# Interleaved high and low parts of split weights, and other start places of the token rows, in a hybrid decoder layer

## The chip, the cores and the metric

The kernel runs on one core of one Trainium2 chip. The metric is device time in microseconds (us) of one execution, the median of several runs. The core has five engines that run side by side: TensorE (PE in the profile; its weight loads are shown apart as PEld), VectorE (DVE), ScalarE (ACT), GpSimd (POOL) and SyncE (SP), which here only starts transfers. Sixteen DMA engines move data between HBM and the on-chip memory, which has 128 partitions. TensorE writes its results into accumulator banks (PSUM), from which VectorE and ScalarE take them.

## The reference

One layer of a decoder, for 4096 new tokens of one sequence and 8 times 8 sampled tokens, all float32 with a model width of 1024:

```
h = rmsnorm(x) * g_pre
z = h @ w_in                  # 1024 x 2816, columns for three groups
A: silu(cg) * cb * conv3(cc * ch)                      # gated short convolution, 256 channels
B: silu(ag) * window attention(q, k, v; sink)          # 8 query heads, 2 key heads, window 128
C: silu(mg) * cross attention(mq; 256 memory tokens)   # 4 heads
y = concat(A, B, C) @ w_out   # 1024 x 1024
x + rmsnorm(y) * g_post
```

Beside y for both sets of tokens it returns the last keys, values and convolution inputs, and the memory's keys and values. The kernel keeps float32 accuracy in the large products.

## The kernel before

**Split operands.** [...] A product of two such operands is three matmuls: high with high, high weight with low row, low weight with high row; the product of the two low parts is left out. `product` (line 370) makes them for one 128-wide group of output columns, 260 token columns and the four 128-deep slices of one half of the model width: 12 matmuls, all issued by line 375, each with a weight load of its own. The weights are the operand that is loaded into the array (128 columns), the token rows are streamed through it (260 columns).

**Input projection, 0 to about 935 us.** The 4160 tokens are cut into 8 blocks of 520, and the 22 groups of 128 columns of `w_in` into 11 pairs, which are treated in three phases: four pairs in each of the first two, three in the last. In most blocks a block and a pair are multiplied by a scheme with seven products in place of eight (Strassen's, Winograd's form), for which sums and differences of the weights and of the rows are made ahead; the first two blocks of the first phase use the eight plain products instead. A step is one product of the scheme for all pairs of the phase. In each step TensorE runs 48 matmuls (36 in the third phase), VectorE and ScalarE add the results into the z tiles (`evict`, line 378), and the operand of the next step is split (`split`, line 363: the high part on ScalarE, line 365, the low part on VectorE, line 366). In the third phase attention work of the first tokens stands between the products.

**Where the operands lie.** Each weight tile has 128 partitions and in each of them 1024 numbers, the 512 high parts and then the 512 low parts (`w_slot`, line 174). The tiles of the first three pairs come from the pool `wa`, those of the fourth from the pool `wb`. In the built program the tiles of `wa` begin at a multiple of 256 bytes, those of `wb` 32 bytes below one. `w_split` (line 181) fills a tile: ScalarE casts the high parts (line 182), VectorE subtracts (line 186). In the first phase 17 operations of VectorE (line 605) put whole weights together again from both parts. The split rows lie in tiles of four slices with 320 numbers each, 1280 bytes or five times 256, of which 260 are used. Where in the 320 they begin is set by `begins` (line 355): for two steps that follow each other, the high parts begin 8 or 16 numbers (32 or 64 bytes) and the low parts 40 or 48 numbers (160 or 192 bytes) in. All tiles of rows begin at a multiple of 256 bytes.

**The rest, 935 us to the end.** Attention units and the output projection (line 1501) alternate on TensorE. In the output projection the token rows are the loaded operand, and the weights `wo` are streamed, 512 columns at a time. The tiles of `wo` are made on line 908, in the same pool `wa`, but not by `w_slot`: they are filled by `w_split` too.

The order of the work on each engine is the order in which the program is written where `tc.keep_in_program_order` or the manual schedule holds it, and a scheduler's elsewhere.

Of the kernel before, what the change touches and what calls it, by code (L numbers as in the profile page):

```python
# [9 lines left out]
F32R = mybir.dt.float32r  # L10
# [5 lines left out]
P = 128  # L16
# [36 lines left out]
def hybrid_layer(ctx: ExitStack, tc: tile.TileContext, a: dict):  # L53
# [30 lines left out]
    wa = ctx.enter_context(tc.tile_pool(name="wa", bufs=3 * NP_))  # L84
    pa = ExitStack()
    wb_stack = ExitStack()
    wb = wb_stack.enter_context(tc.tile_pool(name="wb", bufs=NP_, side="right"))
# [84 lines left out]
        return tp.tile([P, wide + 2 * HW], F32, tag="t", name=name)  # L172

    def w_slot(qi, name):
        return (wa if qi < 3 else wb).tile([P, 2, 512], F32R, tag="w", name=name)

    def w_raw(pair, o):

# [173 lines left out]
                tc.keep_in_program_order(ins)  # L352
            store(hd[b][o], ops[o])

    begins = {"hi": [8, 16], "lo": [40, 48]}

    def split_tile(tag, name):

# [239 lines left out]
    def first_fill(o, q, raw=None):  # L598
        ws[0, q, o] = w_slot(q, f"w0_{q}{o}")
        w_split(ws[0, q, o], raw0.pop((q, o)) if raw is None else raw)  # L600
# [273 lines left out]
    def next_fill(nph, q, o):  # L874
        ws[nph, q, o] = w_slot(q, f"w{nph}_{q}{o}")
        w_split(ws[nph, q, o], raws.pop((q, o)))
# [815 lines left out]
```

## Time and profile before

| | before |
|---|---|
| median of 3 runs | 1540.98 us (1539.1 to 1541.51) |
| profiled execution, and its span | 1543.23 us, 1541.5 us |
| mean granted TensorE clock | 0.998 |
| PE, PEld, DVE, ACT, POOL busy | 99%, 91%, 74%, 52%, 25% of the span |
| matmuls of the input projection (line 375) | 7488, 54.7% of the chain of waits |
| matmuls of the output projection (line 1501) | 22.5% of the chain of waits |

The profile gives for every instruction its engine, its source line, its start and its length. Matmuls are pipelined: the length of one (282 ns for 260 columns) holds its way through the array and says little of the rate, which is read from the distance between the starts of two, or from a stretch of the chain of waits over many. The chain of waits follows the work that ended last back to what released it, and so names what set the time at each moment. PEclk is the share of TensorE's clock that was granted in a stretch.

### The profile page before, as it was taken

Reading aid. Unit: us, or ns where it says so; the run is one execution under the profiler, and the core shown is the slowest. Engines: PE = TensorE matmul, PEld = TensorE weight load, DVE = VectorE, ACT = ScalarE, POOL = GpSimd, SP = SyncE. Lnnn points to the kernel's source line nnn. Section 1 sums busy time; section 2 is a strip of 40 time slices with the busy share of each in tenths; the row PEclk is TensorE's granted clock in tenths of the full one; section 3 lists DMA queues with packets and bytes.
Section 4 is the critical chain, followed back from the end, with each engine's and each line's share of the span. In section 5 each row is a group of like instructions: output and inputs, shape, how many; then the busy total and the mean of one; then the engine's idle time right before and its main releaser. Section 6 shows DMA issues by size and latency. Waiting matters only on the chain.

```text
span 1541.5 us, 30150 instructions
## 1 busy us (share of the span) xinstructions
PE 1529.6 (99%) x11331; PEld 1407.2 (91%) x11331; DVE 1147.0 (74%) x2055; ACT 806.8 (52%) x2039; POOL 380.8 (25%) x604
## 2 busy tenths in 40 slices
PE   9999999999999999999999999999999999999998
PEld 9999999999999999999999998788888888888877
DVE  6779888898988777887787678766666666666643
ACT  6776566476222222354454447665566556555632
POOL 0223332211400000000101203544444444444310
PEclk9999999999999999999999999999999999999999
DMA  9989999778755333678777789976767676776433
GB/s 267 195 215 242 268 281 268 272 240 290 193 180 180 126 125 126 216 221 286 232 264 229 227 293 257 225 161 155 158 148 148 148 155 157 155 159 152 130 109 96
DMA packets 177942, 306.28 MB, mean 199 GB/s; under 512 B 33925, under 2 KB 107653, under 8 KB 177765
## 3 DMA queue, kind: packets, MB, share of 16 engines
q1 hardware_dynamic: 130901, 227.38, 47.5%
q0 software_dynamic: 46176, 75.92, 24.0%
q8 instruction: 90, 1.47, 0.4%
q10 hardware_dynamic: 720, 1.05, 0.2%
q14 instruction: 55, 0.45, 0.1%
HBM read 197.23 MB, written 108.05 MB: 198 GB/s over the span
## 4 chain that ended last, share of the span: by engine, by line
PE 93%; DVE 3%; DMA 2%; issue 1%; ACT 0%; POOL 0%; DVEq 0%; SPq 0%; POOLq 0%; ACTq 0%
PE c L375 55%; PE y L1501 22%; PE ws L1255 4%; PE wo L1097 2%; PE wt L1278 2%; PE xs L1191 2%; PE xt L1206 2%; PE wo L1227 2%; PE wo L1233 1%; PE mem_acc L798 1%; DMA qd<-z 1%; DVE z L382 0%; DMA wr_1A<-in_w_in 0%; DMA xr<-in_x_p 0%; DVE wo L186 0%
## 5 line engine op out<-in xcount | busy, mean ns | idle before, releaser
L1501 PE MATMUL y<-wo,mh 128*128 128x512 f32 (+1 forms) x1040 | 350.8, 400 | 0.0
L382 DVE TENSOR_TENSOR z<-c,z 128x520 f32<-128x520 f32 (+1 forms) x308 | 194.5, 644 | 94.3 <-PE c L375 92.5
L1501 PEld LDWEIGHTS y<-wo,mh 128*128 128x128 f32 x1040 | 194.5, 188 | 39.3 <-issue 2.4
L1501 PE MATMUL y<-wo,ml 128*128 128x512 f32 (+1 forms) x520 | 201.8, 388 | 0.0
L1268 ACT ACTIVATE sm<-sm,wnm 128x128 f32<-128x128 f32 x256 | 99.6, 391 | 60.8 <-DVE wnm L1262 59.3
L1200 POOL TENSOR_SCALAR xp<-xp,xrd 128x256 f32<-128x256 f32 x128 | 74.9, 593 | 209.2 <-DVE xrd L1196 209.2
L1501 PEld LDWEIGHTS y<-wo,ml 128*128 128x128 f32 x520 | 98.2, 189 | 16.5
L1192 DVE TENSOR_REDUCE xmx<-xs 128x2 f32<-128x512 f32 x64 | 44.1, 689 | 59.7 <-PE xs L1191 59.6
L1280 ACT COPY wpt<-wt 128x512 f32<-128x512 f32 x64 | 37.3, 583 | 88.9 <-PE wt L1278 86.4
L1255 PEld LDWEIGHTS ws<-kst,q 128*128 128x128 f32 x512 | 70.3, 191 | 5.6 <-ACT xp L1195 0.7
L1508 DVE TENSOR_TENSOR yn<-y,gpost 128x512 f32<-128x512 f32 (+1 forms) x66 | 45.0, 682 | 39.9 <-PE y L1501 39.6
L1255 PE MATMUL ws<-kst,q 128*128 128x256 f32 x512 | 73.7, 284 | 0.4 <-ACT xp L1195 0.4
L1509 ACT ACTIVATE y<-y 128x512 f32<-128x512 f32 (+1 forms) x66 | 38.6, 585 | 64.1 <-DVE yn L1508 64.1
L746 POOL CAST wmask<-negs 128x256 uint8<-128x256 f32 x1 | 1.0, 1037 | 267.2 <-DMA negs<-in_wmask 267.2
L1288 POOL TENSOR_SCALAR_AFFINE_SELECT wpt<-wpt 128x512 f32<-128x512 f32 x64 | 52.8, 825 | 42.2 <-ACT wpt L1280 39.2
L1195 ACT ACTIVATE xp<-xs,xnm 128x256 f32<-128x256 f32 x128 | 59.0, 465 | 7.1 <-DVE xnm L1193 7.1
L1130 POOL DMA_DIRECT2D q<-qd x64 | 42.9, 675 | 70.7 <-DVE wo L186 60.9
L1519 DVE SCALAR_TENSOR_TENSOR xr<-yn,yst,xr 128x1024 f32<-128x1024 f32 (+2 forms) x34 | 43.5, 1281 | 15.5 <-POOL yst L1515 13.4
L1119 POOL DMA_DIRECT2D kst<-qd x64 | 38.7, 617 | 63.8 <-PE xt L1206 41.5
L1258 DVE COPY_PREDICATED sm<-wmask,ws 128x256 f32<-128x256 uint8 x124 | 52.1, 436 | 2.5 <-ACT sm L1257 2.3
L1285 POOL TENSOR_SCALAR_AFFINE_SELECT wpv<-wpt 128x512 f32<-128x512 f32 x62 | 40.4, 652 | 52.1 <-ACT wpt L1280 52.0
L384 ACT COPY z<-c 128x520 f32<-128x520 f32 (+1 forms) x44 | 24.4, 554 | 52.9 <-PE c L375 50.0
(962 smaller groups left out, 5121.4 us busy)
## 6 DMA issues: line engine op xcount, KB each, us to landing
q<-qd POOLq DMA_DIRECT2D x64, 384.0 KB, 7.2
xr<-in_x_p SPq DMA_DIRECT2D x32, 512.0 KB
nat<-in_x_p SPq DMA_DIRECT2D x39, 416.0 KB
o_yp<-xr SPq DMA_DIRECT2D x31, 512.0 KB
md<-th POOLq DMA_DIRECT2D x48, 260.0 KB, 6.3
qd<-zh SPq DMA_DIRECT2D x48, 260.0 KB
qd<-z SPq DMA_DIRECT2D x48, 260.0 KB
kst<-qd POOLq DMA_DIRECT2D x60, 192.0 KB, 5.9
```

The source lines that it names most:

```text
L375: TE.matmul(bank[:, :HW], l, r, start=first and i == 0, stop=last and i == 3 * KH - 1)
L382: add = lambda dst, other: V.tensor_tensor(dst, c, other, op=ALU.add)
L1192: V.tensor_reduce(mx[:, :nb], s, axis=AX.X, op=ALU.max)
L1195: S.activation(p[:, i, :], s[:, i, :], AF.Exp, bias=nm[:, i : i + 1], scale=SCALE, accum_out=den[:, i : i + 1])
L1200: G.tensor_scalar(p[:, i, :], p[:, i, :], rd[:, i : i + 1], 0.5, op0=ALU.mult, op1=ALU.mult)
L1255: TE.matmul(s3[:, hh, :], self.q[:, 4 + 2 * (2 * half + hh) + kvh, i * P : i * P + P], self.kst[:, 2 * kvh + part, i * P : i * P + 2 * P], ...
L1258: V.copy_predicated(sm[:, 2 * half : 2 * half + 2, :], third["wmask"], third["negs"] if first else s3[:, :, 0:P])
L1268: S.activation(sm[:, hh, :], sm[:, hh, :], AF.Exp, bias=nm[:, hh : hh + 1], scale=SCALE, accum_out=den[:, hh : hh + 1])
L1288: G.affine_select(p3, p3, pattern=[[0, 4], [1, P]], compare_op=ALU.is_ge, fill=0.0, base=0, channel_multiplier=-1)
L1501: TE.matmul(acc, self.hl[l][:, k], wo[k][c0 // 512][:, r, c0 % 512 : c0 % 512 + c1 - c0], start=j == 0, stop=j == passes * KT - 1)
L1508: V.tensor_tensor(yn[:m, c0:c1], acc[:m], gpost[:m, c0:c1], op=ALU.mult)
L1519: V.scalar_tensor_tensor(self.xr[:m, cs], yn[:m, cs], st[:m, 3:4], self.xr[:m, cs], op0=ALU.mult, op1=ALU.add)
```

## The change

Two places are edited. A weight tile now holds the two parts of each weight next to each other: high, low, high, low. `w_slot` makes the tile with the part as the last dimension and hands out a view in the old order, so that no other line changes: `w[:, 0]` and `w[:, 1]` are now every second number, and every weight load of line 375, every cast of line 182 and difference of line 186 into these tiles, and every read of line 605 goes at a step of two numbers (8 bytes). The tiles of `wo` keep the old order. The rows' begins become 0 or 16 numbers (0 or 64 bytes) for the high parts and 32 or 48 (128 or 192 bytes) for the low ones. On every engine the same instructions stand in the same order as before, the tiles have the same sizes, and the same work is computed.

```diff
@@ -172,7 +172,7 @@
     def w_slot(qi, name):
-        return (wa if qi < 3 else wb).tile([P, 2, 512], F32R, tag="w", name=name)
+        return (wa if qi < 3 else wb).tile([P, 512, 2], F32R, tag="w", name=name).rearrange("p n a -> p a n")
@@ -352,7 +352,7 @@
-    begins = {"hi": [8, 16], "lo": [40, 48]}
+    begins = {"hi": [0, 16], "lo": [32, 48]}
```

## The prediction

> **What bounds the kernel now.** I read the page's engine table first, then the chain of waits, then that chain and the busy time in single stretches. The engine table:
>
> ```profile
> PE 1529.6 (99%) x11331; PEld 1407.2 (91%) x11331; DVE 1147.0 (74%) x2055; ACT 806.8 (52%) x2039; POOL 380.8 (25%) x604
> ```
>
> TensorE never rests, and there is one weight load for every matmul. The chain of waits (start, length, what) puts 54.7% of the span on line 375, the products of the input projection, nearly without a break:
>
> ```profile
> 113.80 238.98 PE c L375 x1992
> 355.91 305.13 PE c L375 x2542
> ```
>
> 305.13 us / 2542 is 120.0 ns from one matmul to the next; 238.98 / 1992 is 120.0 ns too. So the projection is a stream of matmuls of 260 columns at one rate, and the kernel's time there is their number times that rate. The busy time of line 375 in its whole stage gives the number, 7488:
>
> ```profile
> 0.00:935.00 935.00, 906.94 (x7488) 901.54 (x7488) 1.00 0.74 226
> ```
>
> Is 120 ns what the array needs? One short stretch answers it, in which the granted clock was half (window, PE busy, PEclk, DMA share, GB/s), and the same kinds of matmul in the chain within it and at full clock later:
>
> ```profile
> 965.80:969.10 3.30, 3.30 (x15) 0.50 1.20 271
> ```
> ```profile
> 966.74 0.85 PE ws L1255 x4
> ...
> 968.02 0.85 PE xt L1206 x4
> ```
> ```profile
> 1010.01 0.95 PE ws L1255 x8
> ...
> 1015.34 0.44 PE xt L1206 x4
> ```
>
> At half clock a 256-column matmul (line 1255) takes 0.85 / 4 = 213 ns, at full clock 0.95 / 8 = 119 ns. Were it the array's work alone, full clock would give 106. A 128-column transpose (line 1206) takes 213 ns and 110 ns: that one does halve. Its 128 columns are half of the other's and it takes the same 213 ns, so what it waits for is the weight load: about 107 to 110 ns of full clock for 128 columns. Hence in the projection two things of nearly one length run side by side, the rows' stream (260/256 of 106 = 108 ns) and the next weight load (107 to 110), and together they take 120. Some 10 to 12 ns of each matmul go to neither. They appear only when both read on-chip memory at full clock. I read them as the two reads getting in each other's way. The wide matmuls of the last stage show it too: 2.78 / 12 = 232 ns where 512 columns would take 213.
>
> ```profile
> 1007.23 2.78 PE y L1501 x12
> ```
>
> That it depends on addresses is seen in the third phase, where the two places of the token rows alternate from step to step, 36 matmuls in each:
>
> ```profile
> 842.85 4.32 PE c L375 x36
> ...
> 847.62 4.24 PE c L375 x36
> ```
>
> 120.0 and 117.8 ns, in turn. Two per cent hang on where the rows start.
>
> [...]
>
> **The change part by part.** No instruction is added, removed or moved, on any engine or queue. Two things differ.
>
> First, the addresses of the streams. Before, a weight load reads 512 contiguous bytes of each partition in about 107 ns, while the rows' stream reads 1040 bytes in 108: the rows run through memory twice as fast, and gain some 530 bytes on the weights in every matmul. Whatever their distance at the start, they pass through every alignment within 256 bytes twice. That fits the rows: nearly the same 120 ns for all start addresses. After, the load steps over 1024 bytes in the same time. Both streams then run at one speed, and their distance within a matmul is what it was at its start: 0, 64, 128 or 192 bytes (modulo 256) plus a constant. A collision is then either avoided throughout or met throughout.
>
> What a matmul then costs isn't in the trace; nothing on TensorE reads at a step of two. From below it is bounded by the weight load alone, 109 ns: 11 ns less. From above, the nearest row is the half-clock one: if each element came at half the rate, 213 ns, 93 more. Between: if collisions go by the bytes swept, which double, 12 ns more. With distances fixed I take the case of mostly avoided collisions, and of the 11 ns half, as one of the four starts, and the weights of each block's fourth column pair in the first two phases (they lie in another pool, at another alignment), may still collide: 114.5 ns, 5.5 less.
>
> [...]
>
> Can the rest of the kernel follow? The stages (us, then PE, PEld, DVE, ACT, POOL busy, PEclk, DMA share, GB/s):
>
> ```profile
> 100.00:200.00 100.00, 99.89 (x834) 99.69 (x833) 86.68 (x103) 62.91 (x111) 31.82 (x49) 1.00 0.94 250
> 200.00:400.00 200.00, 199.84 (x1668) 199.63 (x1667) 176.35 (x223) 119.38 (x206) 56.26 (x83) 1.00 0.87 252
> 400.00:676.00 276.00, 276.00 (x2303) 275.81 (x2302) 224.92 (x314) 85.34 (x107) 3.90 (x6) 1.00 0.49 170
> 676.00:936.00 260.00, 259.72 (x2112) 253.49 (x2110) 191.95 (x305) 128.52 (x236) 21.47 (x33) 1.00 0.77 251
> ```
> ```profile
> 6.00:200.00 194.00, 192.79 (x1584) 191.92 (x1585) 1.00 0.94 244
> ```
>
> At 114.5 ns the 200 us from 200 become 191, with VectorE busy for 176: still covered, though at 109 ns (182 us) nothing would be left. Before 200 us the DMA engines are at 0.94, and 4.6% less time would ask 0.98 of them. There I count half of the gain.
>
> Second, the writes and re-reads of the weights by the other engines, now at a step of two. Line 182 on ScalarE (81 of these 97 are projection weights, 16 the output weights, which keep their layout), line 186 on VectorE, and the 17 re-reads of line 605:
>
> ```profile
> 0.00:935.00 935.00, 55.41 (x97) 1.00 0.74 226
> ```
> ```profile
> 0.00:935.00 935.00, 61.45 (x95) 1.00 0.74 226
> ```
> ```profile
> 0.00:935.00 935.00, 11.31 (x17) 1.00 0.74 226
> ```
>
> That is 0.57 to 0.67 us each. No such write at a step of two is in the trace. If nothing changes, the cost is 0; if they take twice as long, about 46 us on ScalarE and 63 on VectorE, spread over a stage in which VectorE is idle for 930 - 748 = 182 us:
>
> ```profile
> 6.00:936.00 930.00, 747.71 (x1059) 1.00 0.74 226
> ```
>
> In the tightest part it has 23.65 us idle and 17.92 us of line 186, so even doubled they fit at today's rate of TensorE:
>
> ```profile
> 200.00:400.00 200.00, 17.92 (x28) 1.00 0.87 252
> ```
>
> Only the first splits stand bare, ahead of the first products (timeline):
>
> ```profile
> 5.39 0.62 ACT L182 CAST w_0A<-wr_0A 128x512 fp32r<-128x512 f32 x1
> ```
> ```profile
> 6.04 0.69 DVE L186 TENSOR_TENSOR w_0A<-wr_0A,w_0A 128x512 fp32r<-128x512 f32 x1 [0.25 <-ACT w_0A L182]
> ```
> ```profile
> 6.06 0.58 PE L375 MATMUL c<-hi_0B,w_0A 128*128 128x260 f32 x1 [0.52 <-ACT w_0A L182]
> ```
>
> Doubled, that is at most 1.3 us for each of the two tiles that TensorE waits for, under 3 us in all. I take 0: these engines' rates here (0.62 us for 512 elements) leave 1.2 ns for each element, three times the 0.41 ns (106 / 256) of TensorE's rows. The row tiles of lines 365 and 366 are written as before, 32 bytes further up or down; no row prices a start, and I take 0 for that too.
>
> The sum: 5904 matmuls after 200 us x 5.5 ns = 32.5 us, and 1584 before x 5.5 / 2 = 4.4 us; together 36.9 us less. The profiled execution took 1543.23 us (span 1541.5, and 1.7 around it), which gives 1506.3. The median of the runs, 1540.98, lies 2.25 below the profiled one, so the predicted time is 1504 us.
>
> **The rivals.** *Slower: the collisions grow with the bytes that the load sweeps.* The place is line 375, the price up to the same again as today's 12 ns: 7488 x 12 = 90 us, 1631; if two of the four distances meet, half of it, 1586. It decides from a mean above 120.4 ns. For it: a fixed distance that is bad stays bad for a whole matmul, where today every distance averages out; the four starts are spread evenly over 256 bytes, which avoids no zone that is wider than 64. Against it: the third phase shows that one start of two is already better than the average.
>
> *Slower by far: the load itself takes twice as long at a step of two*, and stands alone on the path: 7488 x 93 = 696 us, 2237. For it is only that no strided load is in the trace; the 0.62 us casts don't bear on it.
>
> *No change: the 12 ns don't come from addresses*, but from something that any load at full clock costs, such as a fixed exchange of weights. Then all stays at 120, 1541 us, give or take 3. For it: the 120.0 ns, equal to a tenth in two phases whatever the start. Against it: 117.8 in the third, and the 232 of the wide matmuls, 19 above theirs where 12 would be due. [...]
>
> **How the numbers follow.** Forecast (faster): 0.48; its own range is from 1468 (all 11 ns but the DMA-bound stage's half: 82 - 9 = 73 us less) to 1525 (the 117.8 ns of the better place everywhere, 16 us less). No change: 0.10. Collisions grow: 0.36. Doubled load: 0.06. About 0.2% is what a measurement of this kernel can tell from no change, 3 us; the chances are faster 0.48, same 0.10, slower 0.42. The range that should hold 8 in 10 reaches from 1468 to 1631: below it is a twentieth, above it the doubled load and a little of the growing collisions. It is wide since the price of one matmul can't be read anywhere, and is paid 7488 times.
>
> **What would show it.** In the chain, line 375 at 114 to 116 ns from matmul to matmul (now 120.0), with steps of different row places further apart than today's 120.0 and 117.8, since distances no longer average out. Line 1501 must stay at 232 ns: the output weights keep their layout. Line 182's casts and line 186's differences at 0.62 and 0.69 us show the writes to be free. VectorE's busy time stays at 1147 us and its share of the stage from 200 us rises above 0.9; new waits of TensorE for DMA before 200 us would show the limit assumed there. A mean above 120 ns on line 375 proves the forecast wrong in its main term; weight loads much longer than today's 188 ns (row below) would point to the load, equal ones to the collisions.
>
> ```profile
> L1501 PEld LDWEIGHTS y<-wo,mh 128*128 128x128 f32 x1040 | 194.5, 188 | 39.3 <-issue 2.4
> L375 PEld LDWEIGHTS c<-hi_1B,w_0A 128*128 128x128 f32 x96 | 15.6, 188 | 0.0
> ```

## The result and the profile after

The changed kernel takes 1548.43 us (median of 4, 1548.11 to 1548.86) against 1540.6 us before: 1.0052 times the time before, 95% interval 1.0035 to 1.0069. It is slower by half a per cent, where 1504 us and a gain were forecast. It lies inside the stated range of 1468 to 1631 us, but on the side of the gain's rivals.

The engine table of its page, to be held against the first row of the prediction:

```profile
PE 1537.3 (99%) x11331; PEld 1415.1 (91%) x11331; DVE 1146.6 (74%) x2055; ACT 809.4 (52%) x2039; POOL 379.9 (25%) x604
```

The counts are the same. TensorE is busier by 7.7 us in matmuls (1529.6 to 1537.3) and 7.9 us in weight loads, and ScalarE by 2.6 us. The chain of waits of the changed kernel (start, length, what) says where:

```profile
87.07 269.22 PE c L375 x2221
...
359.42 310.04 PE c L375 x2556
...
851.03 4.32 PE c L375 x36
855.79 4.37 PE c L375 x36
860.60 4.33 PE c L375 x36
...
1012.83 2.78 PE y L1501 x12
```

269.22 us / 2221 is 121.2 ns from one matmul to the next, and 310.04 / 2556 is 121.3, where it was 120.0. In the third phase the steps of 4.24 us (117.8 ns) are gone. The output projection, whose weights kept their layout, stays at 2.78 / 12 = 232 ns. The busy time of line 375 in the stretch that holds the projection in both kernels, in the windows of after and then of before:

```profile
0.00:950.00 950.00, 916.08 (x7488) 911.07 (x7488) 1.00 0.74 223
```
```profile
0.00:950.00 950.00, 906.94 (x7488) 901.54 (x7488) 1.00 0.75 226
```

That is 9.1 us more. Added up from the starts of the matmuls, all distances within line 375 come to 902.2 us before and 911.1 after: 8.9 us, or 1.2 ns for each of the 7488. This is the loss; nothing else has moved by as much. (The two profiled executions differ by only 5.6 us: the one before lay 2.6 us over the median of 1540.6, and holds the stretch at half clock from 965.7 to 969.1 us, which no other run of this study shows at the start of the output projection.)

The high part of a number is its cast to the type float32r, the low part what the cast leaves. The instructions of single lines in the changed kernel (count, then shortest, median and longest in ns, then the time of the first and the last):

```profile
L182 ACT CAST wo<-wor x16: 613/617/622, 923.1 to 940.9; 128x512 fp32r<-128x512 f32 x16
...
L182 ACT CAST w_0A<-wr_0A x9: 654/663/676, 5.2 to 687.6; 128x512 fp32r<-128x512 f32 x9
...
L186 DVE TENSOR_TENSOR w_0A<-wr_0A,w_0A x9: 686/690/696, 5.9 to 688.9; 128x512 fp32r<-128x512 f32 x9
...
L375 PEld LDWEIGHTS c<-hi_1B,w_0A x96: 193/196/199, 54.6 to 709.8; 128*128 128x128 f32 x96
```

And the same three of the projection in the kernel before:

```profile
L182 ACT CAST w_0A<-wr_0A x9: 606/617/620, 5.4 to 680.8; 128x512 fp32r<-128x512 f32 x9
...
L186 DVE TENSOR_TENSOR w_0A<-wr_0A,w_0A x9: 675/682/693, 6.0 to 682.1; 128x512 fp32r<-128x512 f32 x9
...
L375 PEld LDWEIGHTS c<-hi_1B,w_0A x96: 187/188/192, 54.0 to 702.8; 128*128 128x128 f32 x96
```

A weight load is recorded 8 ns longer (188 to 196). A cast into an interleaved tile is 46 ns longer in these rows (617 to 663), and 54 ns on average over all 81 of them (617 to 671); the casts of `wo`, into the old layout, stay at 617 (615 before). A difference is 8 ns longer (682 to 690), and the 17 re-reads of line 605 are no longer than before (11.24 us, 11.31 before). These writes are not what slows TensorE: in the whole changed kernel it waits 0.4 us for one of them (0.5 before), and the last cast into an interleaved tile ends at 693 us, while the steps of the third phase after that are longer too. The stage from 200 us in the changed kernel (us, then PE, PEld, DVE, ACT, POOL busy, PEclk, DMA share, GB/s):

```profile
200.00:400.00 200.00, 199.88 (x1651) 199.68 (x1650) 175.79 (x220) 119.08 (x206) 54.58 (x81) 1.00 0.88 257
```

TensorE is as full as before (199.84 us then). In 200 us it only gets through 1651 matmuls in place of 1668.

### The profile page after: what moved, and what is told of

The parts are those of the page before. It is cut to its first block, busy times and chain, and to the rows that moved or that the text cites. A ratio compares the mean times of both kernels' runs of the same rounds, so it can differ in the third digit from the quotient of the medians.

```text
span 1547.1 us, 30150 instructions
## 1 busy us (share of the span) xinstructions
PE 1537.3 (99%) x11331; PEld 1415.1 (91%) x11331; DVE 1146.6 (74%) x2055; ACT 809.4 (52%) x2039; POOL 379.9 (25%) x604
## 4 chain that ended last, share of the span: by engine, by line
PE 94%; DVE 2%; DMA 2%; issue 1%; ACT 0%; POOL 0%; DVEq 0%; POOLq 0%; ACTq 0%; SPq 0%
PE c L375 56%; PE y L1501 22%; PE ws L1255 4%; PE wo L1097 2%; PE wt L1278 2%; PE xs L1191 2%; PE xt L1206 2%; PE wo L1227 2%; PE wo L1233 1%; PE mem_acc L798 1%; DMA qd<-z 1%; DVE z L382 0%; DMA wr_1A<-in_w_in 0%; DMA xr<-in_x_p 0%; DVE wo L186 0%
## 5 line engine op out<-in xcount | busy, mean ns | idle before, releaser
L384 ACT COPY z<-c 128x520 f32<-128x520 f32 (+1 forms) x44 | 24.4, 554 | 55.4 <-PE c L375 52.9
```

## The experiments

All kernels below are edits of the kernel before or of the changed one; where a line number is one or two higher, the edit has added lines. A time "per matmul" is a piece of the chain of waits over its count. Where it says "without pauses", it is the mean distance of the starts of two matmuls that follow each other, with the few distances of more than 170 ns left out. A time without an interval is a single execution.

### Which of the two edits

Theory at this point: the rows' new places or the collisions of the two streams are to blame; the rival is the load itself. The first kernel has the interleaved weights and the old places:

```diff
-        return (wa if qi < 3 else wb).tile([P, 2, 512], F32R, tag="w", name=name)
+        return (wa if qi < 3 else wb).tile([P, 512, 2], F32R, tag="w", name=name).rearrange("p n a -> p a n")
```

> The interleaved weight tiles alone; the token rows begin where they did before (32, 64, 160, 192 bytes). Theory A (the two streams' distance decides): with the load at a step of two each distance has its own price, so this differs from the changed kernel (1548.4) by several us, and the means of line 375 for the two row places lie further apart than the 120.0 and 120.3 ns of the kernel before. Theory B (120 ns is the sum for any load at full clock, wherever it reads, and the places only stir it): 1541 to 1548, and the triples of matmuls of the first three weight pairs at 360 ns again.

Measured: 1553.54 us, 1.0089 times before (1.0076 to 1.0103). Line 375 in its windows and the longest piece of its chain:

```profile
0.00:950.00 950.00, 920.44 (x7488) 915.24 (x7488) 1.00 0.73 222
```
```profile
360.44 359.47 PE c L375 x2950
```

The second has the new places and the old layout:

```diff
-    begins = {"hi": [8, 16], "lo": [40, 48]}
+    begins = {"hi": [0, 16], "lo": [32, 48]}
```

> The other start places of the rows alone (0, 64, 128, 192 bytes), weights in two halves as before. If the layout makes the change slower, this is level with the kernel before, 1538 to 1543; if the rows' places make it, 1546 to 1550. A guess from the parts: the weights of the fourth pair, which lie 32 bytes off, are at 118 and 121 ns before and 123 and 122 after; if that comes from their distance to the rows, this run shows it too.

Measured: 1536.58 us, 0.9985 (0.9976 to 0.9994). Its windows, and one of the longest pieces of its chain:

```profile
0.00:950.00 950.00, 902.51 (x7488) 896.60 (x7488) 1.00 0.75 228
```
```profile
480.64 226.09 PE c L375 x1895
```

So the interleaved layout alone costs 14 us (121.9 ns per matmul) and the places alone give back 3 (119.3), a little more than expected. Together they would make +0.7%; the change has +0.5%. The layout is what makes it slower. The first kernel lies outside the 1541 to 1548 us of theory B and 5 us off the changed kernel, as theory A asks. Its two row places are 1.1 ns apart (122.2 and 121.1 without pauses, in the first three pairs), which leaves open whether a distance is held.

### Does a distance that is held matter?

The prediction let the interleaved load and the rows run at one speed, so that their distance would be held through a matmul and would decide its length. Then a walk of the rows' start through all 16 places of 256 bytes must show places that are far quicker and others that are far slower, in the interleaved layout only:

```diff
-    begins = {"hi": [8, 16], "lo": [40, 48]}
+    begins = {"hi": list(range(0, 64, 4)), "lo": [n ^ 32 for n in range(0, 64, 4)]}
...
-        begins[tag].reverse()
+        begins[tag].append(begins[tag].pop(0))
```

> Weights in two halves as before; the start of the rows goes in 16-byte steps through all 16 places of 256 bytes, one after the other from step to step (low parts always 128 bytes from the high ones). Theory A: the mean of line 375 by place varies little, 117 to 122 ns, since the streams pass through every distance. Theory B: 120.0 at most places. Total 1535 to 1550 us.

> The same walk over 16 places with the interleaved weights. Theory A, equal speeds hold a distance: some places near 110 ns and others at 130 or more, a spread of over 15 ns. Theory B: the same narrow band as with the old layout, 117 to 125 ns, with 120.0 most frequent. Total 1535 to 1570 us.

Measured: 1541.8 and 1549.51 us. The longest pieces of the two chains, old layout, then interleaved:

```profile
356.70 354.64 PE c L375 x2950
```
```profile
359.87 357.51 PE c L375 x2950
```

120.2 and 121.2 ns. Sorted by the place of the high rows (worked out from the starts of all matmuls, pauses left out), first three pairs:

```
layout         mean of 16 places   quickest            slowest
old            120.0 ns            118.2 (64 bytes)    122.0 (112 bytes)
interleaved    121.06 ns           119.9 (176 bytes)   122.75 (32 bytes)
```

No place is near 110 or 130 ns. Both layouts spread over the same 3 to 4 ns, about means that are 1.1 ns apart. The theory of held distances falls: the interleaved weights cost a little at nearly every place.

### Stilling one stream, and spreading the load

If neither place nor sweep is the cause, what are the ten ns above 110? In the next two kernels one of the streams reads a single number over and over, first the load, then the rows; its values are left out, and only the time counts.

```diff
             for l, r in ((w[:, 0, ks], h[0][:, k]), (w[:, 0, ks], h[1][:, k]), (w[:, 1, ks], h[0][:, k])):
+                l = l[:, 0:1].to_broadcast([P, P])
```

> Kernel before, but every weight load of line 375 reads one number 128 times (a step of zero): the weights' values are left out, the count of instructions and columns is as before. If reading the weights out of memory beside the rows costs the 10 to 12 ns, they go: 109 to 111 ns a matmul, 1460 to 1475 us. If 120 ns is a fixed sum for any load at full clock: 120, 1541 us.

Measured: 1531.69 us. The longest piece of the chain, 118.6 ns per matmul:

```profile
113.23 236.34 PE c L376 x1992
```

```diff
+                r = r[:, 0:1].to_broadcast([P, HW])
```

> Kernel before, but the rows' stream of line 375 reads one number 260 times: the rows' values are left out. The same question from the other side: 109 to 111 ns if the two reads meet in memory (1460 to 1475 us), 120 ns if the sum is fixed.

Measured: 1504.63 us, with two pieces of 112.1 ns:

```profile
112.46 67.17 PE c L376 x599
...
471.47 166.69 PE c L376 x1487
```

Stilling the load hardly helps; stilling the rows takes away nearly all (the time falls by less than expected, for the other engines then set the pace in places, see below). So most of the extra length is in the rows' stream, whether the load sweeps beside it or not.

A small part does need both. Without pauses a matmul takes 119.7 ns in the kernel before and 118.4 with the load stilled. In the first two phases the two row places, with the first three pairs and with the fourth, spread from 117.9 to 120.8 ns before, and with the load stilled from 118.3 to 118.5: what hangs on the places goes when the load stands still.

The next three, in the old layout, spread the load over more bytes: a step of four, eight and three numbers, so that other weights are multiplied and only the time counts. (In the diff the step of three; the others read 128 numbers at their step in the same way.)

```diff
-            for l, r in ((w[:, 0, ks], h[0][:, k]), (w[:, 0, ks], h[1][:, k]), (w[:, 1, ks], h[0][:, k])):
+            whole = w.rearrange("p a n -> p (a n)")
+            for i0, r in ((128 * k, h[0][:, k]), (128 * k, h[1][:, k]), (256 + 128 * k, h[0][:, k])):
+                l = whole[:, i0 : i0 + 3 * (P - 1) + 1 : 3]
```

> Kernel before with its weight tiles, but each load of line 375 reads 128 numbers at a step of four (one number of each 16 bytes, 2048 bytes swept); which weights are multiplied is left out. If the price goes by lines or bytes swept: step one 120.0, step two 121.1 in the walk over places, so 123 here, 1560 us. If a step of two is the last that memory serves at full rate: 150 ns or more, up to 213, 1770 to 2240 us. If steps don't matter: 120.

> The same at a step of eight (4096 bytes swept, every second line of 16 bytes). By bytes swept: 127 ns, 1595 us. By 16-byte lines touched: as at a step of four. If steps don't matter: 120, 1541 us.

> Kernel before with its weight tiles, but each load of line 375 reads 128 numbers at a step of three (96 lines of 16 bytes, 1.33 numbers in each; which weights are multiplied is left out). If the price goes by the lines that a load touches while it still keeps its pace (1 line 118.4, 32 lines 120.0, 64 lines 121.1 ns): 122 to 123 ns, 1558 us. If fewer than two numbers in a line slow the load itself, as at a step of four (235 ns for 128 lines): between 150 and 200 ns, 1760 to 2140 us.

Measured: 2399.14, 2451.63 and 1945.43 us. The chain of the steps of three, four and eight:

```profile
119.60 905.65 PE c L377 x5196
```
```profile
157.85 1223.10 PE c L377 x5196
```
```profile
162.45 1258.03 PE c L377 x5196
```

174.3, 235.4 and 242.1 ns; the step of four costs more than any reading expected. Up to a step of four numbers, which is 16 bytes, the price goes with the bytes that the load sweeps (58.1 and 58.9 ns for each number of the step, at three and at four). Past it the price stands nearly still, though the bytes double (235.4 and 242.1 ns). So it is counted here in pieces of 16 bytes (the lines of the expectations): 128 numbers touch 96, 128 and 128 of them, which makes 1.82, 1.84 and 1.89 ns for each. The piece and its pace of 1.82 to 1.84 ns are estimates from these three runs. By them a contiguous load touches 32 pieces, 59 ns, which doesn't show; one at a step of two touches 64, 118 ns, just over the 112.1 ns that a matmul takes with a contiguous load and stilled rows. At a step of three the matmul is already at 174.3 ns; a step of two itself is not quite free, as the run with stilled rows below shows (117.9 against 112.1 ns).

### Which place is best, and the fourth pair

With the old layout, the 64-byte place was the best of the walk. Here the rows begin there in every step:

```diff
-    begins = {"hi": [8, 16], "lo": [40, 48]}
+    begins = {"hi": [16, 16], "lo": [48, 48]}
```

> Weights in two halves as before, and one place for the rows in every step: 64 bytes for the high parts, 192 for the low ones. In the walk over the places this one had 118.2 ns with the first three pairs and 120.3 with the fourth. If a place keeps its price when every step uses it: 118.6 ns on average, 1.1 to 1.4 us per thousand matmuls less than before, 1529 to 1532 us. If the price hangs on the change between two places: 1536 to 1541.

Measured: 1531.94 us, 0.9946 (0.9932 to 0.996). The longest piece of the chain, 118.7 ns:

```profile
112.06 236.46 PE c L375 x1992
```

By pairs it is 117.9 ns for the first three and 120.3 for the fourth, whose weights lie 32 bytes below a multiple of 256. The next kernel also brings those to a multiple of 256, by a pad of 56 numbers in their pool's side, 32 spare numbers less in the tile `place`, and the begins moved by 128 bytes so that the absolute places stay:

```diff
+    wb_stack.enter_context(tc.tile_pool(name="pad", bufs=1, side="right")).tile([P, 56], F32, name="pad")
...
-    place = ctx.enter_context(tc.tile_pool(name="place", bufs=1)).tile([P, 2 * KH * HW + 32], F32, name="place")
+    place = ctx.enter_context(tc.tile_pool(name="place", bufs=1)).tile([P, 2 * KH * HW], F32, name="place")
...
-    begins = {"hi": [8, 16], "lo": [40, 48]}
+    begins = {"hi": [48, 48], "lo": [16, 16]}
```

> The same, and the weight tiles of the fourth pair moved by 32 bytes, so that all begin at a multiple of 256 bytes. If the distance from weights to rows sets the price, the fourth pair falls from 120.3 to 118.2 ns: 1368 matmuls x 2.1 ns = 2.9 us less than without the move, 1526 to 1529 us. If it is the tile or the pair, no difference.

Measured: 1529.43 us, 0.9929 (0.9915 to 0.9944), the quickest kernel of this study that does the whole work. Its chain and its windows:

```profile
112.41 203.69 PE c L376 x1727
```
```profile
0.00:950.00 950.00, 892.99 (x7488) 887.00 (x7488) 1.00 0.76 230
```

117.9 ns, now in the fourth pair too (120.3 to 117.9). The same edit to the changed kernel:

> The changed kernel with the fourth pair's tiles moved to a multiple of 256 bytes; the rows at 0, 64, 128 and 192 as there. If the distance sets the price, the fourth pair falls from 122.6 to 120.6 ns: 2.7 us less than the changed kernel, 1545 to 1547 us. The rest of its loss, the step of two, stays: it is not level with the kernel before.

Measured: 1544.78 us, 1.0029 (1.002 to 1.0039); the fourth pair goes from 122.6 to 120.0 ns. A long piece of its chain, at 120.4 ns:

```profile
114.68 239.90 PE c L376 x1992
```

So in either layout the place of the weights against the rows is worth 2 to 3 ns, and the fourth pair's 32 bytes are not what makes the change slower. To see whether the interleaved weights do as well at a place of their own, both of their better places were held in every step, again with the fourth pair brought in line: 0 bytes (`{"hi": [32, 32], "lo": [0, 0]}` in the moved numbers) and 176 bytes (`{"hi": [12, 12], "lo": [44, 44]}`).

> Interleaved weights, all weight tiles at a multiple of 256 bytes, and one place for the rows in every step: 0 bytes for the high parts, 128 for the low ones, 120.0 ns in the walk over the places. If the layout loses at its best place too: 120.0 to 120.4 ns, 1541 to 1545 us, not below the kernel before. If one place alone frees it, as 64 bytes did with the old layout: under 119 ns, 1535 us or less.

> The same at 176 bytes for the high and 48 for the low parts, the lowest place of the walk with interleaved weights (119.9 ns). Same two readings: 1540 to 1544 us if the layout loses everywhere, 1535 or less if a place frees it.

Measured: 1543.34 us, 1.002 (1.0011 to 1.0029), and 1543.62 us, 1.0021 (1.0013 to 1.003). A long piece of the chain of each:

```profile
113.78 239.34 PE c L376 x1992
```
```profile
113.96 239.35 PE c L376 x1992
```

120.2 ns (120.0 without pauses) in both, 2.2 above the old layout's best, and slower than the kernel before.

### The load's pace without the rows

The changed kernel with the rows at a step of zero:

> The changed kernel, with the rows' stream of line 375 reading one number 260 times (the rows' values are left out). The same with the weights in two halves gave 111.7 ns a matmul and 1504.6 us. If the step of two costs by meeting the rows' stream in memory: 111.7 again, 1504 us. If the load at a step of two is itself longer: about 113 ns, 1510 us or more.

Measured: 1530.39 us. Its longest piece:

```profile
112.36 203.68 PE c L376 x1727
```

117.9 ns, where the old layout had 112.1 with stilled rows and some 113 were expected. Beside the load's step only the place of the one number that the rows read differs, so the interleaved load by itself needs 117.9 ns: by the count above, 64 pieces of 1.84. The instructions of the load there, then with the old layout:

```profile
L376 PEld LDWEIGHTS c<-hi_0B,w_0A x96: 195/197/337, 5.7 to 664.1; 128*128 128x128 f32 x96
```
```profile
L376 PEld LDWEIGHTS c<-hi_0B,w_0A x96: 186/190/190, 5.7 to 648.5; 128*128 128x128 f32 x96
```

The recorded length of the load shows it as well, by 7 ns.

### The rows' pace

This left the rows. 260 contiguous numbers from a multiple of 16 bytes are 65 pieces; if the load's pace, an estimate, held for them too, they would need 118 to 120 ns by themselves, and most of the ten ns were never a collision. Three last kernels change the rows' pieces alone, at the price of other values: half as many (130 numbers, each read twice in a row), twice as many (a step of two, the same half of the numbers two times over), and twice as many beside interleaved weights.

```diff
+                r = r[:, : HW // 2].rearrange("p (n o) -> p n o", o=1).to_broadcast([P, HW // 2, 2])
```

> The kernel before, with the rows of every product matmul of the projection read as 130 numbers, each twice in a row: still 260 columns, but 520 bytes, 32.5 lines of 16 bytes, so the values are other ones and only the time counts. Theory that the rows' stream has a pace of its own of 1.82 to 1.84 ns for a line (65 lines, 118 to 120 ns, in the kernel before): 33 lines need 60 ns, which is less than the columns need, so the matmul falls to the 111.7 ns of the rows at a step of zero, with the same waits behind it, 1503 to 1508 us. Rival, the streams' collisions by the bytes that they sweep: half of the bytes, half of the 8 ns, 115 to 116 ns, 1515 to 1522 us. Rival, a fixed cost of any sweep: 118 to 120 ns, 1530 to 1541 us.

```diff
+                r = r[:, 0 : HW - 1 : 2].rearrange("p (o n) -> p o n", o=1).to_broadcast([P, 2, HW // 2])
```

> The kernel before, with the rows of every product matmul read at a step of two numbers, the same half of them twice over: 260 columns, 130 lines of 16 bytes with two numbers used in each; the values are other ones and only the time counts. Theory of a pace for each line: 130 x 1.82 to 1.84 = 237 to 239 ns, 2400 to 2430 us. Rival, collisions of two streams that are quick by themselves: at most the 12 ns again, 132 ns, 1631 us. Rival, one port that both reads share line by line: 130 + 32 lines, 295 to 298 ns, 2840 to 2870 us.

> The changed kernel, with the same rows at a step of two numbers, so that rows (130 lines) and weights (64 lines) both go at a step of two; the values are other ones and only the time counts. Two ports, each with its own pace: the longer one sets it, 237 to 241 ns as with contiguous weights, 2400 to 2440 us. One shared port: 194 lines, 353 to 357 ns, 3270 to 3300 us. Collisions of quick streams: under 135 ns, under 1655 us.

Measured: 1500.42, 2389.62 and 2386.83 us, each a little under the time expected. The chains in this order:

```profile
466.83 166.69 PE c L376 x1487
```
```profile
156.11 1215.12 PE c L376 x5196
```
```profile
156.79 1211.74 PE c L376 x5196
```

Half the pieces: 112.1 ns, to the hundredth of a us the 166.69 of the rows at a step of zero, although they sweep 520 bytes. Twice the pieces: 233.9 ns, which is 130 pieces of 1.80, a little under the 237 expected. And with interleaved weights 233.2: the load's 64 pieces beside the rows' 130 add nothing. Neither collisions (at most 132 ns expected) nor one shared port (295 and 353 ns expected) fit. In these runs the two reads go side by side, and to within a few ns the longer one counts: 118.6 ns for the rows with the load stilled, 117.9 for the interleaved load with the rows stilled, 121.2 for both in the changed kernel, 233.2 for both with the rows at a step of two. That the rows' piece is 16 bytes is taken over from the load, an estimate: half, once and twice the pieces are also half, once and twice the bytes swept (112.1, 120.0 and 233.9 ns), and no run parts the two for the rows.

## Why the prediction was wrong

**What TensorE waits for in the projection: misread, and this carried the rest.** The step was "Some 10 to 12 ns of each matmul go to neither. ... I read them as the two reads getting in each other's way." The runs put this in its place: the rows need 118.4 to 118.6 ns by themselves, with the load stilled; counted in 65 pieces of 16 bytes, the estimate above, that is some 1.82 ns for each, and 1.81 at the best place (117.9). The extra length is in the rows' stream (118.6 ns with the load stilled), it goes with half the pieces (112.1), and with twice the pieces the matmul takes about twice as long (233.9). The two reads do get in each other's way, but by 1.3 ns on average and not by 10 to 12 (119.7 ns without pauses, 118.4 with the load stilled). The short stretch at half clock had misled: there 256 columns take 213 ns, longer than the 116 that their 64 pieces would take at 1.81 ns by this estimate, so a limit that is in the pieces does not show, and half of 213 is no proof that full clock could have 106. (Had the pieces slowed with the clock, it would have been 232 ns there.) The wide matmuls, quoted but put down to the collisions, fit it: 232 ns over 512 / 4 = 128 pieces is 1.81 ns. A collision fits less well, as the prediction noticed itself (19 ns where 12 would be due).

**"With distances fixed I take the case of mostly avoided collisions ... 114.5 ns, 5.5 less": the term of the sum that failed.** It measured 1.2 ns more (36.9 us less were forecast, 8.9 us more came). There was next to nothing to avoid: the rows took 118.4 ns without the load's sweep, and 117.8 to 122.75 with the first three pairs in either layout and at any place. Nor did held distances spread the places: within 3 to 4 ns in both layouts.

**The load "109 ns" from below, "213" from above: the mechanism named as a rival, at a far smaller size.** "The load itself takes twice as long at a step of two" is the right place with the wrong price: 117.9 against 112.1 ns with the rows stilled, 6 ns and not 93. A price of that order comes only beyond a step of two (174.3 ns at three, 235.4 at four).

**Where the 1.2 ns lie.** Most of the load's 6 ns is hidden beside the rows, and by the longer stream alone the change would have cost next to nothing: 118.4 ns for the rows without the load's sweep, 117.9 for the interleaved load without the rows'. Together they take 120.9 (without pauses), 2.5 more than the longer of them; in the kernel before it was 119.7, 1.3 more than the rows' 118.4. So the loss is in what the two streams take from each other when both sweep, and this grew by 1.2 ns with the load from 32 to 64 pieces. (The 1.3 and the 2.5 are good to about half a ns, since at its best place the old layout is at 117.9 with both sweeping; their difference is the measured loss.) No place of the walk takes it away: at its better places the interleaved layout runs at 120.0 ns, the old one at its best at 117.9. Whether it grew because the load has more pieces or because the two streams are now of one length, no run shows; beside rows of 130 pieces the interleaved load costs nothing (233.2 against 233.9).

**"The collisions grow with the bytes swept"**: right sign for the time, and right that the two streams cost each other more, but at a fifth to a tenth of the price: 8.9 us, where 45 to 90 were put down. Its condition, a mean above 120.4 ns, was met (121.2). That they grow with the bytes is not shown. **"No change"** came nearest in us, for reasons that don't hold: 117.9 to 123 ns can be had by addresses alone, and the interval of the result (1.0035 to 1.0069) excludes no change.

**The rows' new places** got no term of their own beside the collisions. Alone they gave 3 us (0.9985), which hides a part of the layout's 14.

**The work of the other engines: right in the sum, and wrong in size by little.** Line 182's casts were put at 0 and took 46 to 54 ns more, 3.2 us of ScalarE's busy time in the projection (55.4 to 58.6 us); line 186's took 8 ns more. VectorE's busy time stayed at 1147 us, and no wait came of it. The reason given, that 1.2 ns for each element leave room, doesn't hold for ScalarE.

**Cover at a quicker rate: right in kind.** The prediction saw VectorE and the DMA engines without slack at 109 to 114 ns. With stilled rows the matmuls save 7488 x 8 ns = 60 us by their rate (119.7 to 111.7 without pauses), and the time falls by 35.5. The chain's shares on the profile page of that kernel, and two of TensorE's longer waits (us in total, times, longest):

```profile
PE 72%; DMA 8%; DVE 7%; issue 4%; ACT 1%; POOL 1%; SPq 0%; DVEq 0%; POOLq 0%; ACTq 0%
```
```profile
PE c L376 <- DVE lo_0B L366: 2.1, 3, 1.4
PE c L376 <- DVE lo_2T L366: 1.7, 2, 0.9
```

TensorE ends last in 72% of the span (94% in the changed kernel), with the splits of the rows and the transfers in its place. By the same share, 35.5 of 60, the forecast 114.5 ns would have brought some 24 of its 7488 x 5.5 ns = 41 us, and not 36.9; this is an estimate.

**The signs to look for**: line 1501 stayed at 232 ns, as said. The steps of the third phase came no further apart but closer (120.0 to 121.4 ns in turn, where 117.8 and 120.0 stood). VectorE's share of the stage from 200 us stayed at 0.88, and the profile shows no wait of TensorE for a transfer. Of the weight loads the prediction said that much longer ones would point to the load, equal ones to collisions; 196 against 188 lay between; the run with stilled rows shows that the load is longer.

**Still open**: how the places of weights and rows move a matmul by up to 4 ns when both streams sweep, why so many averages settle at just 120.0, and why the 64-byte place costs 119.9 ns in the first two phases of the kernel before, where it alternates with 32, but 117.9 where it stands alone or alternates with 0, and 117.8 in the third phase, where it alternates with 32 as well. So the distance modulo 256 bytes is not the whole of it.

## What to carry to other kernels

Count the pieces of 16 bytes that each of TensorE's two reads touches, at about 1.8 ns a piece by the estimate here, beside the 112.1 ns that 260 columns and a contiguous load took with the rows stilled: the longest of the three gave the pace of line 375 in all of these runs, to within some 5%. Contiguous rows of 260 numbers already set the pace by themselves in this kernel (118.6 ns with the load stilled, 112.1 with half of their pieces), so that a step in the weights had little to win there, and lost. Before a gap above the arithmetic is put down to contention, still one stream, then the other: what each takes alone, and what both take together, tells contention from a stream's own pace, and two cheap kernels would have told it ahead of any layout work. Where rows and weights stand to each other within 256 bytes is worth a scan, since one line of code and an alignment pad took 0.7% off a kernel whose TensorE is 99% busy.

## What the runs showed of the hardware beyond that

At full clock a matmul of 260 columns of contiguous float32r rows took 117.9 ns at best, and 112.1 when as many columns touched half the bytes: the type alone did not bring the rows to that rate. Matmuls with loads at a step of two (rows stilled), three and four numbers took 117.9, 174.3 and 235.4 ns, 58 to 59 ns for each number of the step, and at a step of eight only 3% more. Writing 512 numbers at a step of two, ScalarE took 7 to 9% longer (617 to 663 ns, 671 on average), VectorE 1% (682 to 690).
